# A hybrid trunk block on one core: 512-column products in the value projections, the FFN and the down projection

## The chip, the cores and the metric

The kernel runs on one core of one Trainium2 chip. The metric is the device time of one execution in microseconds (us), as the median of several runs. One run is also recorded by the hardware profiler, and its trace is read below.

## The reference, cut to what matters

One layer over 256 tokens of width 1024, batch 1, in float32. One input projection of the normed input feeds four token mixers and their gates; the gated mixers are summed and projected, and a SwiGLU FFN follows.

```
h = rmsnorm(x, norm_mix)
z, xbc, dt, qkvB, qkvC, f, qD, kvD, gates = split(h @ w_in)      # w_in: 1024 x 9488
A = mamba2(z, xbc, dt)            # 8 heads of 64, state 128, one chunk of 256 tokens
B = moba(qB, kB, vB, bias)        # 8 heads of 64; causal attention with a relative bias
C = fox(qC, kC, vC, f)            # 8 heads; logits less a running sum of log forget gates
D = swa(qD, kD, vD, bias, sinks)  # window of 128
m = sum over b of sigmoid(gate_b) * (branch_b @ w_branch[b])
x = x + m @ w_out
u = rmsnorm(x, norm_ffn)
x = x + (silu(u @ w_gate) * (u @ w_up)) @ w_down                 # width 2816
out = rmsnorm(x, norm_final)
```

## The kernel before

**Products in parts.** Each float32 operand of a projection is split into a high part and a low part, and a product becomes three: hi\*hi, hi\*lo and lo\*hi. The names of the parts end in h and l (xh, xl: the normed input; x2h, x2l: the FFN's input; ah, al: the FFN's inner activations) or begin with hi and lo (the weights). `three` (line 259) writes the list of terms. Before the change each of the three is an instruction of its own.

**Weight stream.** Weights come from DRAM in 1 MB pieces, in the order of `stream()`: the pieces of FIRST, then gates (g) and branch projections (wb), the output projection (wo), 22 FFN pieces (gu) and 11 pieces of the down projection (dn). SyncE (SP) issues the loads into three buffers `raw`; ScalarE (ACT) copies the high part (line 299) and VectorE (DVE) subtracts for the low part (line 307), each in two cuts. A piece of FIRST, and one of gu, holds 256 columns over the whole contraction of 1024. Its products run on TensorE (PE) as two halves of 24 products with 256 columns each (line 249 in the input projection, line 1106 in the FFN). A gate piece holds 512 columns over half the contraction, and its products are 512 columns wide (line 961). A piece of the down projection makes, for the first 128 tokens, two products of 512 columns, and for the second 512, 256 and 256 (line 1131).

**Side work.** Everything else (convolution, attention, norms, ends of the pieces) is written as generators. The `Weaver` (line 92) advances them between the halves of the projections, by rough costs and flags such as `"qkB0"` or `"erow"`. So the order on every engine is fixed when the program is built, and an engine whose next instruction waits holds all that stands behind it. A pair of heads in `att_pair` (line 720) goes through logits s on PE (lines 731, 733), bias and minimum on DVE (spB, lines 744 and 746), exponentials on ACT (pB), scaling on DVE, transposes on PE (ptB, line 776), copies on ACT (ptsB, line 782), and the product with the values on PE (yB, lines 652 and 654). MoBA's bias rows go through DRAM: ACT copies them (es), SP writes them (erow), and GpSimd (POOL) reads them back per pair (bB, line 557). They become due by this line:

```
    wv.later(lambda: bias_rows(), ["dt"])
```

The flag dt is raised where `softplus_cums` (line 484) is written out; its chain of some twenty small POOL instructions (lines 503 to 524) stands ahead of the bB reads in POOL's own queue.

**FFN end.** `end_ffn` (line 1076) scales both halves of a piece by 1/rms (gs, on DVE, 512 columns), takes the SiLU (sg, ACT), multiplies (DVE), and splits the result into ah (ACT) and al (DVE).

Of the kernel before, what the change touches and what calls it, by code (L numbers as in the profile page):

```python
# [15 lines left out]
EPS = 1e-6  # L16

# Columns of w_in.
# [20 lines left out]
def in_proj_pieces():  # L39
    """(name, columns of w_in) of each piece of the input projection."""  # L40
# [6 lines left out]
    for j in range(2):  # L47
        cols["xbc%d" % (2 + j)] = rng(XS0 + 256 * j, 256)
        cols["z%d" % j] = rng(Z0 + 256 * j, 256)
        cols["vB%d" % j] = rng(BV0 + 256 * j, 256)  # L50
        cols["vC%d" % j] = rng(CV0 + 256 * j, 256)
        cols["qD%d" % j] = dq[256 * j : 256 * j + 256]
# [18 lines left out]
WARM = 8  # L71
SLACK = 3500
# [5 lines left out]
class Need:  # L78
    """What a step of side work takes: rough times on the engines, and buffers by their tags."""
# [12 lines left out]
class Weaver:  # L92
    """Weaves side work into the instruction order of the projections.

    The projections keep the tensor engine busy; between two of their accumulation groups the steps of
    the other work are traced, as far as rough clocks of the engines say that they will not hold it up."""
# [16 lines left out]
    def step(self, t):  # L113
        """Run the task's next step if it fits; whether it did."""
# [49 lines left out]
    def tick(self, cost, last=True):  # L164
        """After a projection's group, or a part of one, that holds the tensor engine for cost."""
# [10 lines left out]
    def until_free(self, tag):  # L176
        """Trace side work until a buffer of this tag is free."""
# [8 lines left out]
    def until(self, flags):  # L186
        """Trace side work until these flags are up."""
# [10 lines left out]
def hybrid_block_kernel(ctx: ExitStack, tc: tile.TileContext, A, out):  # L198
# [45 lines left out]

    def group(o, terms):
        """One accumulation group; the groups of a bank follow each other."""
        n = len(terms)
        for j, (l, r) in enumerate(terms):
            pe.matmul(o, l, r, start=j == 0, stop=j == n - 1)  # L249

    def woven(o, terms, cuts=1):
        """One accumulation group with side work between its cuts."""
        n = len(terms)
        for j, (l, r) in enumerate(terms):
            pe.matmul(o, l, r, start=j == 0, stop=j == n - 1)  # L255
# [3 lines left out]
    def three(w, x, ks, wt, cuts=1):  # L259
        """Terms hi*hi + hi*lo + lo*hi; wt: the weights stand still (else the activations do)."""  # L260
        (wh, wl), (xh, xl) = w, x
        t = []
        step = len(ks) // cuts
        for a in range(0, len(ks), step):
            kk = ks[a : a + step]
            for k in kk:
                t += [(wh(k), xh(k)), (wh(k), xl(k))]
            t += [(wl(k), xh(k)) for k in kk]
        return t if wt else [(b, a) for a, b in t]
# [5 lines left out]
    names = stream()  # L275
    sizes = {n: 8 * len(c) for n, c in in_proj_pieces()}
# [25 lines left out]
    def split_lo(name, c, cuts):  # L302
        """After the last cut, the load of a later piece."""
# [10 lines left out]
    # The cuts of the splits in order; the first parts run one cut ahead of the second.  # L314
# [4 lines left out]
    def split_next(which, least, most):  # L319
        """Trace cuts of one of the two parts up to piece least, and one more cut up to piece most."""  # L320
# [68 lines left out]
    xh = [slot("xh%d" % i, dt=F32R) for i in range(2)]  # L389
    xl = [slot("xl%d" % i, dt=F32R) for i in range(2)]  # L390
# [7 lines left out]
    for a, b in chunks:  # L398
        for k in range(a, b):
            act.activation(xh[k // 4][:, k % 4, :], xT[k // 4][:, k % 4, :], AF.Copy, scale=nm_mix[:, k : k + 1])  # L400
        act.activation(hb[:, a:b, :], wb[:, a:b, :], AF.Copy)
        for k in range(a, b):
            dve.scalar_tensor_tensor(xl[k // 4][:, k % 4, :], xT[k // 4][:, k % 4, :], nm_mix[:, k : k + 1],
                                     xh[k // 4][:, k % 4, :].bitcast(F32), ALU.mult, ALU.subtract)
        dve.tensor_tensor(lb[:, a:b, :], wb[:, a:b, :], hb[:, a:b, :].bitcast(F32), ALU.subtract)
        for w, x in ((hb, xh), (hb, xl), (lb, xh)):
            for k in range(a, b):
                for j in range(2):
                    pe.matmul(px[j], w[:, k, tok(j)], x[k // 4][:, k % 4, :], start=k == 0 and w is hb and x is xh,
# [10 lines left out]
    def rms(name, ss, width):  # L420
        """(ss / width + eps) ** -0.5 of a [128, n] tile of sums of squares."""
# [7 lines left out]
    def rms_row(name, r):  # L429
        """The [128, 2] columns of 1/rms as one row on every partition, in PSUM [128, 256]."""  # L430
# [6 lines left out]
    def nat_groups(name, hi, lo, n=256):  # L437
        """n columns, natural layout: PSUM [128, 2 token halves, 256], or two banks."""
# [5 lines left out]
        for t in range(2):  # L444
            group(p[:, t, :] if n == 256 else p[t],
                  three((lambda k: hb[:, k, :], lambda k: lb[:, k, :]),
                                    (lambda k: xh[k // 4][:, k % 4, tok(t)],
# [815 lines left out]
```

## Time and profile before

| what | value |
|---|---|
| median of three runs | 523.21 us (522.54 to 524.31) |
| profiled execution, span | 522.5 us |
| PE busy | 512.6 us, 98% |
| DVE, ACT, POOL busy | 342.4, 272.6, 31.0 us |
| weights and data read | 94.46 MB, 183 GB/s over the span |

The profiled execution's own time is its span, 0.7 us under the median and just under the fastest of the three runs. PE is busy in all slices but the first and the last. The other engines have idle time, which costs nothing unless PE waits for them.

### The profile page before, as it was taken

Reading aid. Unit: us, or ns where it says so; the run is one execution under the profiler, and the core shown is the slowest. Engines: PE = TensorE matmul, PEld = TensorE weight load, DVE = VectorE, ACT = ScalarE, POOL = GpSimd, SP = SyncE. Lnnn points to the kernel's source line nnn. Section 1 sums busy time; section 2 is a strip of 40 time slices with the busy share of each in tenths; the row PEclk is TensorE's granted clock in tenths of the full one; section 3 lists DMA queues with packets and bytes.
Section 4 is the critical chain, followed back from the end, with each engine's and each line's share of the span. In section 5 each row is a group of like instructions: output and inputs, shape, how many; then the busy total and the mean of one; then the engine's idle time right before and its main releaser. Section 6 shows DMA issues by size and latency. Waiting matters only on the chain.

```text
span 522.5 us, 8748 instructions
## 1 busy us (share of the span) xinstructions
PE 512.6 (98%) x3544; PEld 467.2 (89%) x3544; DVE 342.4 (66%) x624; ACT 272.6 (52%) x471; POOL 31.0 (6%) x61
## 2 busy tenths in 40 slices
PE   7999999999999999999999999999999999999995
PEld 7999999898987778888888899999999999988884
DVE  4478887897968937547295495656656665673435
ACT  6576674665675853443534454755544544443412
POOL 2008110011200000000000000000000000000001
PEclk8999999999999999999999999999999999999999
DMA  7974665553563244726447282446455545575302
GB/s 232 378 266 156 202 208 180 190 149 150 188 215 123 82 161 167 273 109 258 162 161 279 113 327 88 166 162 238 162 173 212 181 162 181 216 289 181 141 1 83
DMA packets 17126, 96.13 MB, mean 184 GB/s; under 512 B 2235, under 2 KB 3563, under 8 KB 6844
## 3 DMA queue, kind: packets, MB, share of 16 engines
q1 hardware_dynamic: 15660, 91.15, 48.0%
q0 software_dynamic: 1424, 4.41, 3.1%
q8 instruction: 28, 0.46, 0.3%
q14 instruction: 14, 0.11, 0.1%
HBM read 94.46 MB, written 1.09 MB: 183 GB/s over the span
## 4 chain that ended last, share of the span: by engine, by line
PE 94%; DMA 3%; issue 1%; SPq 1%; DVE 0%; ACT 0%; POOL 0%; POOLq 0%; ACTq 0%
PE gu L1106 24%; PE pg L961 17%; PE pd L1131 11%; PE pb L255 8%; PE qkC L249 4%; PE qkB L249 4%; PE po L1062 4%; PE xbc L249 3%; DMA raw_xbc<-in_w_dram 3%; PE vC L249 2%; PE qD L249 2%; PE vB L249 2%; PE z L249 2%; PE n L249 1%; PE ptC L776 1%
## 5 line engine op out<-in xcount | busy, mean ns | idle before, releaser
L1106 PE MATMUL gu<-x2h,hi_gu 128*128 128x256 f32 x352 | 87.0, 283 | 0.0
L1106 PE MATMUL gu<-x2l,hi_gu 128*128 128x256 f32 x352 | 86.9, 283 | 0.0
L1106 PEld LDWEIGHTS gu<-x2l,hi_gu 128*128 128x128 f32 x352 | 67.6, 192 | 0.0
L1106 PEld LDWEIGHTS gu<-x2h,hi_gu 128*128 128x128 f32 x352 | 67.6, 192 | 0.0
L307 DVE TENSOR_TENSOR lo_gu<-raw_gu,hi_gu 128x1024 fp32r<-128x1024 f32 x44 | 53.2, 1217 | 1.4 <-ACT hi_gu L299 1.4
L1106 PE MATMUL gu<-x2h,lo_gu 128*128 128x256 f32 x352 | 51.4, 283 | 0.0
L961 PE MATMUL pg<-hi_g,xh 128*128 128x512 f32 x128 | 50.8, 397 | 0.0
L961 PE MATMUL pg<-hi_g,xl 128*128 128x512 f32 x128 | 50.0, 390 | 0.0
L299 ACT ACTIVATE hi_g<-raw_g 128x1024 fp32r<-128x1024 f32 x32 | 32.8, 1053 | 26.8 <-DMA raw_g<-in_w_dram 14.0
L1106 PEld LDWEIGHTS gu<-x2h,lo_gu 128*128 128x128 f32 x352 | 46.3, 192 | 0.0
L299 ACT ACTIVATE hi_gu<-raw_gu 128x1024 fp32r<-128x1024 f32 x44 | 45.4, 1049 | 1.6 <-PE gu L1106 1.6
L307 DVE TENSOR_TENSOR lo_g<-raw_g,hi_g 128x1024 fp32r<-128x1024 f32 x32 | 38.1, 1219 | 8.8 <-ACT hi_g L299 8.8
L1079 DVE TENSOR_TENSOR gs<-gu,rb2b 128x512 f32<-128x512 f32 x22 | 15.1, 690 | 43.9 <-PE gu L1106 43.9
L307 DVE TENSOR_TENSOR lo_dn<-raw_dn,hi_dn 128x1024 fp32r<-128x1024 f32 x22 | 26.1, 1220 | 22.7 <-ACT hi_dn L299 22.7
L1082 ACT ACTIVATE sg<-gs 128x256 f32<-128x256 f32 x22 | 9.1, 419 | 57.9 <-DVE gs L1079 57.9
L1131 PE MATMUL pd<-hi_dn,al 128*128 128x512 f32 (+1 forms) x110 | 37.3, 348 | 0.0
L1131 PE MATMUL pd<-hi_dn,ah 128*128 128x512 f32 (+1 forms) x110 | 37.2, 347 | 0.0
L299 ACT ACTIVATE hi_dn<-raw_dn 128x1024 fp32r<-128x1024 f32 x22 | 22.4, 1051 | 26.4 <-PE pd L1131 24.6
L961 PE MATMUL pg<-lo_g,xh 128*128 128x512 f32 x128 | 34.3, 389 | 0.0
L961 PEld LDWEIGHTS pg<-hi_g,xh 128*128 128x128 f32 x128 | 24.0, 188 | 6.3 <-issue 1.5
L1131 PE MATMUL pd<-lo_dn,ah 128*128 128x512 f32 (+1 forms) x110 | 29.2, 347 | 0.0
L961 PEld LDWEIGHTS pg<-lo_g,xh 128*128 128x128 f32 x128 | 24.0, 188 | 5.1
(332 smaller groups left out, 1201.8 us busy)
## 6 DMA issues: line engine op xcount, KB each, us to landing
raw_gu<-in_w_dram SPq DMA_DIRECT2D x22, 1024.0 KB, 4.8
raw_g<-in_w_dram SPq DMA_DIRECT2D x16, 1024.0 KB, 4.7
raw_dn<-in_w_dram SPq DMA_DIRECT2D x11, 1024.0 KB, 4.8
raw_wb<-in_w_dram SPq DMA_DIRECT2D x8, 1024.0 KB, 4.8
raw_qkB<-in_w_dram SPq DMA_DIRECT2D x4, 1024.0 KB, 5.2
raw_qkC<-in_w_dram SPq DMA_DIRECT2D x4, 1024.0 KB, 4.9
raw_wo<-in_w_dram SPq DMA_DIRECT2D x4, 1024.0 KB, 5.2
raw_vB<-in_w_dram SPq DMA_DIRECT2D x2, 1024.0 KB, 4.8
```

The source lines that it names most:

```text
L249: pe.matmul(o, l, r, start=j == 0, stop=j == n - 1)
L255: pe.matmul(o, l, r, start=j == 0, stop=j == n - 1)
L299: act.activation(parts[name][0][:, s], raws[name][:, s], AF.Copy)
L307: dve.tensor_tensor(lo[:, s], raws[name][:, s], hi[:, s].bitcast(F32), ALU.subtract)
L776: pe.transpose(pt[:, tok(c)], pp[i][:, tok(c)], ident)
L961: pe.matmul(pg[t], l, r, start=kh == 0 and i == 0, stop=kh == 1 and i == len(terms) - 1)
L1062: pe.matmul(po[m], l, r, start=kh == 0 and i == 0, stop=kh == 1 and i == len(terms) - 1)
L1079: dve.tensor_tensor(s, p, rb2b.broadcast_to([128, 2, 256]), ALU.mult)
L1082: act.activation(sg, s[:, 0, :], AF.Silu)
L1106: pe.matmul(p[:, j, :], l, r, start=ks[0] == 0 and i == 0, stop=ks[-1] == 7 and i == len(terms) - 1)
L1131: pe.matmul(pd[t, i], l, r, start=c == 0 and j == 0, stop=c == 10 and j == len(terms) - 1)
```

## The change

**FFN.** For pieces 4 to 21 the input is normed before its products: `normed_x2` makes, for each eighth of the contraction, x2T times norm_ffn times 1/rms, and splits it into x3x, a tile that holds the high and the low part next to each other. `wide` multiplies the high weights by both parts in one product of 512 columns, then the low weights by the high part in 256 columns. The two halves of the 512 columns are added at the end: ACT copies one half out of PSUM (ge), DVE adds the other (gs). Gate and up columns of a piece now have a bank each.

**Values.** A value piece is now half the contraction and 512 columns, like a gate's. Both pieces of a branch stand next to each other in FIRST, and a pair of heads waits for both.

**Down projection.** In pieces 0 to 8 the second 128 tokens also take two products of 512 columns. The last 256 columns of pieces 9 and 10 go into a bank of their own and are added at the end.

**Layout.** The tiles x, y, m, x2 and a hold both parts next to each other; where the products stay as they were, `mm` still issues two of 256 columns.

```diff
-FIRST = ("xbc0 xbc1 n0 qkB0 vB0 xbc2 qkB1 xbc3 vB1 z0 qkB2 z1 qkB3 qD0 qkC0 vC0 qkC1 qD1 qkC2 vC1 qkC3").split()
+FIRST = ("xbc0 xbc1 n0 qkB0 vB0 vB1 xbc2 qkB1 xbc3 z0 qkB2 z1 qkB3 qD0 qkC0 vC0 vC1 qkC1 qD1 qkC2 qkC3").split()
...
+RAW_F = 4
...
+    def wide(o, w, x, ks, start, stop):
+        (wh, wl), n = w, len(ks)
+        for i, k in enumerate(ks):
+            pe.matmul(o, wh(k), x(k), start=start and i == 0, stop=False)
+        for i, k in enumerate(ks):
+            pe.matmul(o[:, 0, :], wl(k), x(k)[:, 0, :], start=False, stop=stop and i == n - 1)
...
+    def normed_x2(k):
+        yield Need(dve=400, act=310, w1=1)
...
+        u = work("x3_%d" % k, [128, 256], "w1")
+        dve.scalar_tensor_tensor(u, x2T[k // 4][:, k % 4, :], nm_ffn[:, k : k + 1], rb2b[:, 0, :], ALU.mult, ALU.mult)
+        h_, l_ = (parts_of(x3x)(k)[:, i, :] for i in range(2))
+        act.activation(h_, u, AF.Copy)
+        yield Need(dve=340)
+        dve.tensor_tensor(l_, u, h_.bitcast(F32), ALU.subtract)
...
     def end_ffn(f, p):
...
+        if f < RAW_F:
+            dve.tensor_tensor(s, p, rb2b.broadcast_to([128, 2, 256]), ALU.mult)
+            rel(acc=1)
+        else:
+            e = work("ge%d" % f, [128, 2, 256], "w2")
+            for j in range(2):
+                act.activation(e[:, j, :], p[j][:, 1, :], AF.Copy)
+                dve.tensor_tensor(s[:, j, :], p[j][:, 0, :], e[:, j, :], ALU.add)
+            rel(acc=1, att=1, w2=1)
...
+        if f >= RAW_F:
+            if f == RAW_F:
+                wv.until(["x3_%d" % k for k in range(8)])
+            p = [(acc, att)[j]("gu%d%d" % (f, j), [128, 2, 256]) for j in range(2)]
+            for j in range(2):
+                wide(p[j], (lambda k: hb[:, k, tok(j)], lambda k: lb[:, k, tok(j)]), parts_of(x3x), range(8), True, True)
+                wv.tick(GROUP)
+            wv.tasks.append(Task(end_ffn(f, p), True))
+            continue
...
         for t in range(2):
-            for i in range(len(pdw[t])):
-                down(c, t, i)
+            for c0 in (0, 512):
+                if c == 0:
+                    pd[t, c0] = att("pd%d%d" % (t, c0), [128, 512])
+                down(c, t, c0, 512, pd[t, c0], c == 0, False)
             wv.tick(GROUP)
...
+            e = c0 + bank.shape[-1]
+            dve.tensor_tensor(y[:, c0:e], bank, y[:, c0:e], ALU.add)
```

The order of the instructions moves at three places that matter below. The first is DVE around the first pair of MoBA heads: spB is the bias step, lo_... the low part of a weight piece, cu, cc and bc the convolution. Before, these rows stand there:

```order
L307 TENSOR_TENSOR lo_vB_661<-raw_vB_497,hi_vB_660 128x1024
L531 COPY cumn<-cum_n 128x32
L576 SCALAR_TENSOR_TENSOR bc_225<-cu_520,cc_523 128x512
L582 MEMSET cu_825 128x2x3
L584 TENSOR_TENSOR cu_825<-xbc_711,rb 128x2x256
L576 SCALAR_TENSOR_TENSOR xs<-cu_655,cc_658 128x512
L307 TENSOR_TENSOR lo_z_741<-raw_z_617,hi_z_740 128x1024 x2
L744 ISA spB_870,nmB_871<-sB_751,bB_747 128x256
```

With the change the same step follows these:

```order
L609 SCALAR_TENSOR_TENSOR bc_224<-cu_477,cc_481 128x512
L615 MEMSET cu_692 128x2x3
L617 TENSOR_TENSOR cu_692<-xbc_581,rb 128x2x256
L339 TENSOR_TENSOR lo_xbc_609<-raw_xbc_474,hi_xbc_608 128x1024
L609 SCALAR_TENSOR_TENSOR bc_225<-cu_497,cc_500 128x512
L777 ISA spB_705,nmB_706<-sB_661,bB_657 128x256
```

The first bias step moves ahead: it now stands right behind the low part of xbc3's first half, before cumn, the convolution xs of xbc2 and the low parts of z0, which came earlier before.

The second place is ACT around the end of piece z0 (zt is its tanh; hi_qkB a high part of qkB3; ptsB the second pair's copies for its product with the values). Before:

```order
L618 ACTIVATE zt_1025<-zh_1023 128x512
L299 ACTIVATE hi_qkB_1029<-raw_qkB_864 128x1024
L782 ACTIVATE ptsB_1032<-ptB_985 128x384
L782 ACTIVATE ptsB_1034<-ptB_989 128x384
L299 ACTIVATE hi_qkB_1029<-raw_qkB_864 128x1024
```

With the change:

```order
L651 ACTIVATE zt_987<-zh_985 128x512
L331 ACTIVATE hi_qkB_992<-raw_qkB_840 128x1024
L638 ACTIVATE cu_889<-cc_892 128x2x256
L331 ACTIVATE hi_qkB_992<-raw_qkB_840 128x1024
L815 ACTIVATE ptsB_1041<-ptB_995 128x384
L815 ACTIVATE ptsB_1043<-ptB_999 128x384
```

The two copies move behind the convolution's tanh of xbc3 (cu) and the second cut of the high part.

The third place is PE in an FFN piece (gu). Before, high and low part of the input alternate under the same weights, and the low weights follow (the end of one half):

```order
L1106 MATMUL gu_3916<-x2h_3271,hi_gu_3819 128x256
L1106 MATMUL gu_3916<-x2l_3273,hi_gu_3819 128x256
L1106 MATMUL gu_3916<-x2h_3270,lo_gu_3820 128x256 x4
L1106 MATMUL gu_3916<-x2h_3271,lo_gu_3820 128x256 x4
L1106 MATMUL gu_3980<-x2h_3270,hi_gu_3883 128x256
```

With the change one half of a piece reads:

```order
L260 MATMUL gu_3781<-x3x_3682,hi_gu_3643 128x512 x2
L260 MATMUL gu_3781<-x3x_3683,hi_gu_3643 128x512 x2
L260 MATMUL gu_3781<-x3x_3684,hi_gu_3643 128x512 x2
L260 MATMUL gu_3781<-x3x_3685,hi_gu_3643 128x512 x2
L262 MATMUL gu_3781<-x3x_3682,lo_gu_3644 128x256 x2
L262 MATMUL gu_3781<-x3x_3683,lo_gu_3644 128x256 x2
L262 MATMUL gu_3781<-x3x_3684,lo_gu_3644 128x256 x2
L262 MATMUL gu_3781<-x3x_3685,lo_gu_3644 128x256 x2
```

Sixteen products of 256 columns have become eight of 512; the eight with the low weights stay.

## Rows read from the trace of the kernel before

**Rows 1.** The page's fourth part: shares of the chain that ended last.

```profile
PE 94%; DMA 3%; issue 1%; SPq 1%; DVE 0%; ACT 0%; POOL 0%; POOLq 0%; ACTq 0%
```

**Rows 2.** That chain in order of time: start us, us, engine and line, instructions.

```profile
39.72 5.76 PE xbc L249 x48
...
46.59 5.76 PE qkB L249 x48
...
67.37 0.44 PE xct L640 x4
...
236.95 21.76 PE pg L961 x96
...
333.99 121.67 PE gu L1106 x1014
455.66 55.34 PE pd L1131 x294
```

**Rows 3.** The same chain between 106 and 126 us, around attention products.

```profile
106.58 0.66 PE ptB L776 x6
107.23 2.87 PE qkC L249 x24
110.10 0.42 PE sB L731 x4
...
110.96 3.06 PE vC L249 x24
...
125.10 0.81 PE ptB L776 x6
```

**Rows 4.** Timeline of POOL: start us, us, instruction, and the wait before it.

```profile
45.68 0.25 POOL L514 TENSOR_TENSOR sp_p<-sp_p,sp_t 128x32 f32<-128x32 f32 x1
...
46.39 1.05 POOL L514 TENSOR_TENSOR sp_p<-sp_p,sp_t 128x32 f32<-128x32 f32 x1
...
52.81 0.20 POOL L524 COPY av<-dt 128x16 f32<-128x16 f32 x1
55.14 1.54 POOL L557 DMA_DIRECT2D bB<-erow  x2 [2.13 <-DMA erow<-es]
```

**Rows 5.** View of the tile bB, MoBA's bias rows: its reader on DVE, its transfers.

```profile
L744 DVE CUSTOM_DVE_ANT_0 spB<-sB,bB x8: 415/418/426, 63.2 to 113.9; 128x256 f32<-128x256 f32 x8
...
DMA to landing us min/median/max: 3.7/3.9/5.2
```

**Rows 6.** Timeline of ACT, 52 to 77 us.

```profile
52.95 0.97 ACT L480 ACTIVATE es<-e 8x384 f32<-8x384 f32 x2
...
70.45 0.63 ACT L605 ACTIVATE cu<-cc 128x512 f32<-128x512 f32 x1 [0.16 <-ACT pB L751]
...
74.86 1.04 ACT L299 ACTIVATE hi_qkB<-raw_qkB 128x1024 fp32r<-128x1024 f32 x1
75.81 0.85 ACT L782 ACTIVATE ptsB<-ptB 128x384 f32<-128x384 f32 x2
```

**Rows 7.** Timeline of DVE, 46 to 84 us.

```profile
46.12 1.22 DVE L307 TENSOR_TENSOR lo_xbc<-raw_xbc,hi_xbc 128x1024 fp32r<-128x1024 f32 x1
47.25 1.67 DVE L603 SCALAR_TENSOR_TENSOR cc<-cu,tapsh,cc 128x256 f32<-128x256 f32 x4
...
82.71 0.87 DVE L643 TENSOR_TENSOR xc<-xct,dt 128x128 f32<-128x128 f32 x4
```

**Rows 8.** Timeline of DVE at the start of the FFN.

```profile
340.26 1.28 DVE L1079 TENSOR_TENSOR gs<-gu,rb2b 128x512 f32<-128x512 f32 x2
...
349.00 1.09 DVE L1088 TENSOR_TENSOR al<-sg,ah 128x256 fp32r<-128x256 f32 x3
...
352.02 0.69 DVE L1079 TENSOR_TENSOR gs<-gu,rb2b 128x512 f32<-128x512 f32 x1 [0.79 <-PE gu L1106]
```

**Rows 9.** Timeline of ACT at the start of the FFN.

```profile
342.28 1.28 ACT L1082 ACT_TABLE_LOAD   x1
```

**Rows 10.** Sixteen FFN pieces: length, then busy us (instructions) of PE, PEld, DVE, ACT, POOL; clock, DMA.

```profile
352.00:444.20 92.20, 92.20 (x770) 92.20 (x770) 58.08 (x81) 43.84 (x64) 0.00 (x0) 1.00 0.52 186
```

More of the change, by code (lines that the diff above doesn't have):

```diff
@@ L254, in woven, with three, two @@
         for j, (l, r) in enumerate(terms):
-            pe.matmul(o, l, r, start=j == 0, stop=j == n - 1)
+            mm(o, l, r, j == 0, j == n - 1)
             if (j + 1) % (n // cuts) == 0:
                 wv.tick(GROUP / cuts, j == n - 1)
-    def three(w, x, ks, wt, cuts=1):
-        (wh, wl), (xh, xl) = w, x
+    def three(w, x, ks):
+        (wh, wl) = w
+        t = []
+        for k in ks:
+            t += [(x(k)[:, 0, :], wh(k)), (x(k)[:, 1, :], wh(k))]
+        return t + [(x(k)[:, 0, :], wl(k)) for k in ks]
+    def two(w, x, ks, cuts=1):
+        (wh, wl) = w
         t = []
@@ L455, in tr_groups @@
         for j in range(n // 128):
-            group(p[:, j, :], three((lambda k: hb[:, k, tok(j)], lambda k: lb[:, k, tok(j)]),
-                                    (lambda k: xh[k // 4][:, k % 4, :], lambda k: xl[k // 4][:, k % 4, :]),
-                                    range(8), True, cuts))
+            group(p[:, j, :], two((lambda k: hb[:, k, tok(j)], lambda k: lb[:, k, tok(j)]), xx, range(8), cuts))
             yield p
@@ L568, in hybrid_block_kernel, with yh, yl @@
     sqa = slot("sqa")
-    yh, yl = {}, {}
+    yy = {}
     def new_y(br):
-        yh[br], yl[br] = slot("yh" + br, dt=F32R), slot("yl" + br, dt=F32R)
+        yy[br] = [slot("y%s%d" % (br, i), (128, 2, 2, 256), F32R) for i in range(2)]
+    def yh(br, j):
+        return yy[br][j // 2][:, j % 2, 0, :]
+    def yl(br, j):
+        return yy[br][j // 2][:, j % 2, 1, :]
     def half_silu(o, h, th):
@@ L850, in end_scaled, with end_v @@
         wv.done.add(name)
-    def end_nat(name, outs, p):
-        yield Need(act=720)
-        for t in range(2):
-            act.activation(outs[t], p[:, t, :], AF.Copy, scale=r1[:, t : t + 1])
+    def end_v(br, t, p):
+        yield Need(act=620)
+        if br not in v:
+            v[br] = slot("v" + br, (128, 2, 512))
+        act.activation(v[br][:, t, :], p, AF.Copy, scale=r1[:, t : t + 1])
         rel(acc=1)
-        wv.done.add(name)
+        wv.done.add("v%s%d" % (br, t))
     def end_of(name, p):
@@ L909, in merged_parts @@
     def merged_parts(nh):
-        mth[nh], mtl[nh] = slot("mth%d" % nh, dt=F32R), slot("mtl%d" % nh, dt=F32R)
+        for kp in range(2):
+            mtx[2 * nh + kp] = slot("mtx%d%d" % (nh, kp), (128, 2, 2, 256), F32R)
         tps = []
@@ L1103, in hybrid_block_kernel @@
                 wv.until(["x2_%d" % k for k in ks])
-                terms = three(w, x, ks, True)
+                terms = two(w, x2x, ks)
                 for i, (l, r) in enumerate(terms):
-                    pe.matmul(p[:, j, :], l, r, start=ks[0] == 0 and i == 0, stop=ks[-1] == 7 and i == len(terms) - 1)
+                    mm(p[:, j, :], l, r, ks[0] == 0 and i == 0, ks[-1] == 7 and i == len(terms) - 1)
                 wv.tick(GROUP * len(ks) // 8, ks[-1] == 7)
@@ L1111, in hybrid_block_kernel @@
                 wv.tasks.append(Task(end_ffn(f_, gu[f_]), True))
+            for k in range(8):
+                wv.tasks.append(Task(normed_x2(k), True))
         gu[f] = p
@@ L1145, in hybrid_block_kernel @@
         o = slot("out%d" % t, (128, 1024))
-        ms, last = EPS, len(pdw[t]) - 1
-        for i, (c0, n) in enumerate(pdw[t]):
+        ends = (((0, 512), (512, 512)), ((0, 512), (512, 256), (768, 256)))[t]
+        ms, last = EPS, len(ends) - 1
+        for i, (c0, n) in enumerate(ends):
             ns = slice(c0, c0 + n)
+            bank = pd[t, c0] if c0 < 768 else att("pd_end", [128, 256])
             for c in (9, 10):
-                down(c, t, i)
+                down(c, t, c0, n, bank[:, :n], c == 9 and c0 == 768, c == 10)
             m = const("ms3_%d%d" % (t, i), [128, 1])
```

131 lines of the change are left out of this document (63 added, 68 removed).

## The prediction

> **What bounds the kernel now.** I read the chain that ended last first. PE holds 94% of it [rows 1], and its pieces follow each other without a gap: the FFN is one piece of 1,014 products, the down projection one of 294 [rows 2]. The windows view says the same of sixteen FFN pieces: PE is busy for all of 92.20 us, at full clock, while DVE works 58.08 and ACT 43.84 of them [rows 10]. So a product that becomes cheaper shortens the time at once, as long as no other engine makes PE wait; a wait that PE does not have today costs its full length. The prediction is therefore a sum of PE's products and of new waits. I looked for these by walking through the changed order with the durations of the trace.
>
> **Products: the gain.** The chain gives two prices. A run of 48 products of 256 columns takes 5.76 us, 120.0 ns each; 96 of 512 columns take 21.76 us, 226.7 ns each [rows 2]. Two of 256 cost 240.0, so one of 512 in their place saves 13.3 ns. The new wide products have weights in the stationary place and the activations moving, the gates' the other way round. The trace has no wide product of that kind, but 256-column products cost the same both ways: 121.67 us for 1,014 in the FFN is 120.0 each [rows 2]. So I take 13.3.
>
> Counted in the two orders, 438 pairs are merged: 288 in the FFN (18 pieces, two halves, 8 pairs), 96 in the four value pieces, 54 in the down projection. 438 x 13.3 ns is 5.83 us: 3.84, 1.28 and 0.72. The bounds are nothing (the saving would be gone if the fixed part belonged to each 256 columns and not to each instruction, which the gates' row contradicts) and 5.83.
>
> **Switches: a small gain.** After logits or a product with values, the next half of 24 products takes 3.06 us instead of 2.87, and a transpose for attention 0.81 instead of 0.66 [rows 3]. The cause is not shown; the price is 0.19 and 0.15. The changed order puts these products next to each other more often. Of logits followed by a projection there are 12 before and after; of value products followed by a projection 7 before and 6 after, by a transpose 6 before and 3 after. That is one of 0.19 and three of 0.15: 0.64 us. Bounds: 0 to 0.64.
>
> **Start of the FFN: covered.** Piece gu4 needs x3x, so 1/rms must be there and 24 new instructions must be done while PE works on gu3. Piece gu3 ends at 352.02, where DVE was waiting for it, and DVE began the first scaling at 340.26 [rows 8]. From there DVE has in the new order, by pitches from start to next start: two scalings at 0.6 (1.28 for two), eight products at 0.40 (cc, 1.67 for four [rows 7]), twelve instructions of 0.335 (al, 1.09 for three [rows 8]: eight low parts, two products, two al), and two cuts of the weights at 1.13 [rows 7]. That is 1.2 + 3.2 + 4.0 + 2.3 = 10.7. It waits about 1.7 for the first SiLU, since ACT loads a table for 1.28 until 343.56 [rows 9]. The last low part stands at about 352.7. PE needs it for the eighth product of gu4, at 352.02 + 7 x 0.227 = 353.6. Cost 0, with 0.9 us of cover; were 2 us more of work in the way, PE would lose 1.1, once.
>
> **Later FFN pieces: covered.** A piece gets shorter, 5.76 to 5.55. DVE has 58.08 / 16 = 3.63 us of work in one and ACT 2.74 [rows 10]. ACT gets two copies of 0.335 more, DVE two additions for one scaling, 0.07 more. 3.7 and 3.4 fit in 5.55, and PE has banks for the next pieces while an end is at work. Cost 0.
>
> **First MoBA pair: a new wait at the head of DVE's queue.** In the first order shown the bias step spB comes earlier. What it reads, bB, cannot come as much earlier. Before, POOL finished its chain at 53.01 and then waited for the rows in DRAM, issued at 55.14, and the transfer landed 3.9 us later (3.7 to 5.2 over the four [rows 5]), at 59.0; DVE read it at 63.2 [rows 4, 5]. With the change es, which ended at 53.92 [rows 6], is copied while PE works on xbc2, by about 49 (an estimate), so only POOL's chain holds the read: issue at about 53.05, landing at 56.95. DVE gets there sooner. The two value pieces in a row begin at 33.96 (one piece before 39.72) and take 48 x 0.227 = 10.9; 1.1 of side products (45.48 to 46.59) and xbc2's 5.76 put its end at 51.7 [rows 2]. One scaling, one cut, one bc later, 2.4 us, DVE stands at spB: 54.1. It waits 2.9 us.
>
> Behind it in DVE's order stand the other cut of xbc3, cumn (PE transposes it and POOL reads its rows for the Mamba pairs), the scaling of pB, and the convolution of xbc2; ACT's tanh of that, a cut and the running sums stand ahead of the copies ptsB. From 56.95 I add on DVE 1.1 for the bias steps [rows 5], 1.13, 0.1, 1.3 for pB (an estimate: six small instructions at 0.2 to 0.3), 0.6, six convolution steps at 0.40 and one cut: 64.7; on ACT tanh 0.54, cut 0.95, row copy 0.3 and two copies of 0.42 [rows 6]: 67.4. PE reaches the first product with the values after four halves (3.06 + 3 x 2.87) and 3.6 of side products at the prices of rows like these [rows 2, 3]: 51.7 + 15.3 = 67.0. So PE waits 0.4. With landing 0.2 earlier it is 0.2, with 5.2 for the transfer 1.7. I take 0.4.
>
> **Second MoBA pair: ACT's copies come late.** In the second order shown both ptsB stand behind tanh cu and a cut. From the end T of z0 on PE, DVE has a scaling 0.6, two convolution steps 0.8, a cut 1.13, four xc 0.85, zs 0.6 and four steps 1.65 [rows 7, 8]: 5.6. Then ACT: tanh 0.55, cut 0.95, two copies 0.85 [rows 6]: T + 8.0. PE has transposes for xc 0.44, two halves of 2.87 and ptB 0.66 [rows 2, 3]: T + 6.8. It waits 1.2 by this, and less where ACT's rows overlap more; I take 1.0, bounds 0.6 to 1.25. Later, one pair of the FoX branch (sC3) comes close as well: 0.25, bounds 0 to 0.35.
>
> **Down projection and end.** One addition on DVE near the end grows from 256 to 512 columns, 0.3 us more, in front of the last one, which waited for PE by about as much. I take 0; bound 0.3.
>
> **Sum.** -5.83 - 0.64 + 0.4 + 1.0 + 0.25 = -4.8. The profiled execution is 522.5, so its like is 517.7; the median is 0.7 above that execution, so the forecast is 518.4. With every bound at its best it is 517.5, with the worst (no switches saved, waits of 1.7, 1.25 and 0.35, tail 0.3) 521.0.
>
> **Rivals.** Differences under about 0.3%, 1.6 us, can hardly be told from no change here: faster means under 521.6, slower over 524.8.
>
> *B, the bias rows come later still.* POOL's chain is sensitive: one of its instructions takes 0.25 us at 45.68 and 1.05 at 46.39, while DVE subtracts a low part at 46.12 [rows 4, 7]. With one or two more such meetings, or a slow transfer, landing moves from 56.95 to 58.5 or 60, and everything behind the bias step moves with it: PE waits 2 to 3.5 instead of 0.4, and the Mamba pairs, which need cumn, may add 0.5. That gives 520.0 to 522.0. Against it: the number of cuts on DVE during the chain is the same before and after. The Trainium skill (SBUF — State Buffer, section "SBUF: two separate sides") has a rule for this: VectorE with two inputs in SBUF and a GpSimd instruction that reads it exclude each other for a whole instruction. By that rule a cut that starts first costs POOL up to its whole 1.1 us; the trace agrees, with 0.8 more.
>
> *C, the saving is not in the instruction.* If a product of 512 in the FFN ran at twice the price of 256, only the switches and the waits would remain: 522.5 - 0.64 + 1.65 + 0.7 = 524.2; with a fifth of the saving left, 523.1. The Trainium skill (TensorE: Matmul & The Clock Gate, section "Back-to-back issue gap") speaks for such a small saving: its gap between products is a term in the columns plus 2.5 ns, so that a merged pair would save 2.5 and not 13.3 ns, 1.1 us in all, an estimate by that page. The trace does not agree: its two prices, 120.0 and 226.7, leave 13.3 for each instruction.
>
> *D, slower: each wide piece has to wait.* A piece now needs two banks, and its end passes between ACT and DVE twice more (ge, then gs). If the banks come free late, PE waits once per piece. From 0.38 us per piece on, 17 x 0.38 = 6.4 takes back all that products and switches save beyond the other waits, 6.5 - 1.65, and another 1.6; at 0.45 it is 526.0 and slower than before. It needs ACT or DVE to have more than 5.55 us of work per piece, or the end to take over a piece's length before it lets go of a bank. The rows say 3.7, and about 1.4 up to the release (two copies, two additions); hence a small chance.
>
> **How the numbers follow.** The sum holds with 0.67 (516.9 to 519.8). B has 0.16, most of it still faster: 0.13, and 0.03 no change. C 0.06, no change. D 0.08, slower; it stands for any wait in the FFN that the walk missed, since 18 pieces repeat it. The last 0.03 is that PE's waits don't come and more is saved: under 516.9. The range from 516.9 to 521.2 holds the first case and nearly all of B, 0.8. Faster: 0.67 + 0.03 + 0.13 = 0.83; same: 0.06 + 0.03 = 0.09; slower: 0.08.
>
> **What would show it.** Right: wide products at 227 ns in the FFN's chain, a piece in 5.55 us, no wait of PE between 352 and the end; DVE idle for about 3 us at its first spB, released by the transfer of bB; PE waiting twice for ptsB, for half a microsecond at about 67 and one at about 82. Wrong: a wide product over 235 ns (C), idle time of PE before gu rows (D or the start), a first spB later than 58 us (B).

## The result, and the profile after

The change took 519.50 us (median of four, 519.36 to 521.76) beside 523.76 for the kernel before: ratio 0.9925, 95% interval 0.9908 to 0.9941, so 3.9 us faster by the ratio (3.1 to 4.8 by its interval) and 4.3 by the medians. The forecast was 518.4 with a range of 516.9 to 521.2. Timed once more in another set, it took 521.72 (nine runs, 518.33 to 522.92) beside 523.89, ratio 0.9950, 0.9934 to 0.9967. That is 2.2 us faster by the medians, and 0.5 above the forecast's range. Why it differs so from run to run is the subject of half of what follows.

The profiled execution has a span of 517.8 us, and its time is 519.55. The chain after, in order of time (start us, us, engine and line, instructions), at the places of [rows 2]; the first row, which has its fellow in the row from the kernel before below it, is the first piece whose products are the same in both:

```profile
21.10 6.02 PE n L250 x48
33.10 10.91 PE pvB L989 x48
...
351.32 1.84 PE gu L260 x8
353.16 0.95 PE gu L262 x8
...
451.88 54.44 PE pd L1186 x240
```

The same row of the kernel before:

```profile
21.97 6.02 PE n L249 x48
```

The reader is to see three things. The profiled execution of the change is 0.87 us ahead before its first changed instruction: the first loads landed earlier, which differs from run to run (that row begins between 21.1 and 22.7 in the profiles of this study). So of the 4.7 us between the two spans only 3.8 belong to the change. The value pieces run at 10.91 / 48 = 227.3 ns a product and the down projection at 54.44 / 240 = 226.8, the gates' price of [rows 2]. The FFN's wide products do not: 1.84 for eight is 230.

The list of PE's waits in the execution after (what waited, for what: us in total, times, longest; the list leaves out waits under 0.15 us), and the windows view of the 18 pieces, as in [rows 10]:

```profile
PE xbc L440 <- ACT hi_xbc L432: 2.3, 2, 2.1
PE warm L424 <- DVE cumu L383: 1.1, 1, 1.1
PE yB L685 <- ACT ptsB L815: 0.9, 1, 0.9
```

```profile
352.00:451.90 99.90, 99.90 (x575) 87.97 (x574) 69.67 (x112) 59.57 (x109) 0.00 (x0) 1.00 0.54 191
```

PE waits once after the start, for the second pair's copies, as forecast. In the FFN it never waits here; DVE has 69.67 / 18 = 3.9 us of work per piece and ACT 3.3, close to what was worked out (3.7 and 3.4).

The first MoBA pair: timelines of POOL and DVE (start us, us, instruction, and the wait before it), which answer to [rows 4]:

```profile
51.39 0.20 POOL L551 COPY av<-dt 128x16 f32<-128x16 f32 x1
51.54 1.54 POOL L584 DMA_DIRECT2D bB<-erow  x2
```

```profile
46.50 1.27 DVE L339 TENSOR_TENSOR lo_qkB<-raw_qkB,hi_qkB 128x1024 fp32r<-128x1024 f32 x1
...
55.98 0.42 DVE L777 CUSTOM_DVE_ANT_0 spB<-sB,bB 128x256 f32<-128x256 f32 x1 [2.66 <-DMA bB<-erow]
```

POOL no longer waits for the rows in DRAM (2.13 us before): its own chain, which ends at 51.59, is what holds the read, and DVE stands 2.66 us at the head of its queue. The forecast said 2.9. The second pair, on ACT's timeline, as in [rows 6]:

```profile
79.94 0.64 ACT L638 ACTIVATE cu<-cc 128x512 f32<-128x512 f32 x1 [3.36 <-issue]
80.48 1.04 ACT L331 ACTIVATE hi_qkB<-raw_qkB 128x1024 fp32r<-128x1024 f32 x1
81.42 0.85 ACT L815 ACTIVATE ptsB<-ptB 128x384 f32<-128x384 f32 x2
```

ACT is idle for 3.36 us ahead of the convolution's tanh (cu), with the two copies behind it, for which PE waits. The row names no releaser; DVE's last steps of that convolution end at 79.85, 0.09 before the tanh begins:

```profile
78.19 1.66 DVE L636 SCALAR_TENSOR_TENSOR cc<-cu,tapsh,cc 128x256 f32<-128x256 f32 x4
```

### The profile page after: what moved, and what is told of

It reads as the page before. It is cut to its first block, busy times and chain, and to the rows that moved or that the text cites. A ratio compares the mean times of both kernels' runs of the same rounds, so it can differ in the third digit from the quotient of the medians.

```text
span 517.8 us, 7989 instructions
## 1 busy us (share of the span) xinstructions
PE 507.6 (98%) x3106; PEld 444.1 (86%) x3106; DVE 350.6 (68%) x658; ACT 284.1 (55%) x511; POOL 29.7 (6%) x61
## 4 chain that ended last, share of the span: by engine, by line
PE 95%; issue 2%; DMA 1%; ACT 1%; DVE 1%; SPq 0%; POOL 0%; POOLq 0%; ACTq 0%; DVEq 0%
PE pg L989 17%; PE gu L260 13%; PE pd L1186 11%; PE pb L250 8%; PE gu L262 7%; PE pvC L989 2%; PE pvB L989 2%; PE qkC L252 2%; PE po L250 1%; PE gu L250 1%; PE gu L253 1%; PE po L253 1%; PE gu L252 1%; PE qkC L250 1%; PE po L252 1%
## 5 line engine op out<-in xcount | busy, mean ns | idle before, releaser
L260 PE MATMUL gu<-x3x,hi_gu 128*128 128x512 f32 x288 | 72.1, 392 | 0.0
L989 PE MATMUL pg<-hi_g,xx 128*128 128x512 f32 x256 | 64.3, 393 | 0.0
L260 PEld LDWEIGHTS gu<-x3x,hi_gu 128*128 128x128 f32 x288 | 51.8, 189 | 9.3
L989 PEld LDWEIGHTS pg<-hi_g,xx 128*128 128x128 f32 x256 | 47.4, 188 | 11.1 <-issue 1.5
L1186 PE MATMUL pd<-hi_dn,aa 128*128 128x512 f32 (+1 forms) x176 | 46.2, 384 | 0.0
L262 PEld LDWEIGHTS gu<-x3x,lo_gu 128*128 128x128 f32 x288 | 39.3, 190 | 2.8
L262 PE MATMUL gu<-x3x,lo_gu 128*128 128x256 f32 x288 | 40.2, 282 | 0.0
L1186 PEld LDWEIGHTS pd<-hi_dn,aa 128*128 128x128 f32 x176 | 32.6, 188 | 6.5
L989 PE MATMUL pg<-lo_g,xx 128*128 128x512 f32 x128 | 34.3, 389 | 0.0
L1186 PE MATMUL pd<-lo_dn,aa 128*128 128x512 f32 (+1 forms) x88 | 26.7, 384 | 0.0
```

Of the source, the lines that this page charges most:

```text
L260: pe.matmul(o, wh(k), x(k), start=start and i == 0, stop=False)
L262: pe.matmul(o[:, 0, :], wl(k), x(k)[:, 0, :], start=False, stop=stop and i == n - 1)
L989: pe.matmul(pg[t], l, r, start=kh == 0 and i == 0, stop=kh == 1 and i == len(terms) - 1)
L1186: pe.matmul(o, l, r, start=start and j == 0, stop=stop and j == len(terms) - 1)
```

## The experiments

All comparisons below by trace are of stretches of PE's work, since the start differs by more than some of the effects. They are: from the first product of piece n to the first of the FFN; from there to the first product of the down projection; and the rest of PE's work. What follows PE's last product is not in the table; it takes 5.9 to 6.0 us in ten profiles and 6.7 in those of e5, e7 and e10, which is taken up at the end of this section. The kernels were timed in four sets, each beside its own runs of the kernel before (medians 523.76, 523.95 for e1 to e4, 524.04 for e5 to e8, 523.89 for e9 to e11), so a ratio says more than a median. "Lost at gu4" is how much longer the first wide products of the FFN take than the same products of later pieces.

| kernel | median us, n | ratio to before (95%) | n to FFN | FFN | rest | lost at gu4 |
|---|---|---|---|---|---|---|
| before | - | - | 305.92 | 127.78 | 61.07 | - |
| the change | 519.50, 4 | 0.9925 (0.9908 to 0.9941) | 306.11 | 124.66 | 60.18 | 0 |
| e1_no_wide_ffn | 523.67, 11 | 0.9994 (0.9986 to 1.0003) | 306.04 | 127.78 | 60.18 | - |
| e2_no_wide_values | 519.75, 6 | 0.9923 (0.9911 to 0.9934) | 306.10 | 124.66 | 60.17 | 0 |
| e3_hi_then_lo | 519.83, 6 | 0.9928 (0.9909 to 0.9946) | 305.84 | 124.86 | 60.18 | 0.6 |
| e4_early_pts | 519.24, 5 | 0.9907 (0.9893 to 0.9920) | 306.98 | 125.92 | 60.18 | 1.3 |
| e5_bias_on_sp | 520.43, 5 | 0.9933 (0.9920 to 0.9946) | 305.73 | 125.71 | 60.18 | 1.0 |
| e6_late_gu4_split | 519.95, 5 | 0.9922 (0.9909 to 0.9936) | 307.60 | 124.66 | 60.18 | 0 |
| e7_all_mended | 518.97, 4 | 0.9901 (0.9887 to 0.9914) | 304.39 | 124.30 | 60.18 | 0 |
| e8_four_and_four | 520.95, 1 | - | 305.91 | 126.15 | 60.18 | 1.0 |
| e9_change_again | 521.72, 9 | 0.9950 (0.9934 to 0.9967) | 306.20 | 125.86 | 60.18 | 1.2 |
| e10_mended_again | 518.73, 4 | 0.9910 (0.9897 to 0.9923) | 304.40 | 124.30 | 60.18 | 0 |
| e11_moves_without_sp | 518.19, 4 | 0.9895 (0.9882 to 0.9908) | 304.68 | 124.30 | 60.17 | 0 |

**One part undone.** First the FFN, then the values.

```diff
-RAW_F = 4
+RAW_F = 22
...
-            for k in range(8):
-                wv.tasks.append(Task(normed_x2(k), True))
```

> The changed kernel with its FFN pieces 4 to 21 in 256 columns as before (no normed copy of the input, no second bank, no halves to add); values and down projection stay wide. Theory: the trace of the change shows 5.587 us per wide piece, so the FFN is worth 18 x 0.171 = 3.1 us and this kernel takes 519.5 + 3.1 = 522.6. By the sum on record (3.84 for the FFN) it takes 523.3. Rival: the new ends on ACT and DVE cost PE something elsewhere (start of the FFN, down projection), then less comes back than 3.1 and it takes under 522.

It took 523.67, no faster than before within its interval. By trace the FFN is 127.78 again, to the hundredth as before: the FFN is worth 3.12, not 3.84. The down projection keeps its 0.89, and the input projection stays 0.12 slower than before. So by trace 0.77 us should be left of the gain, where the medians of this set leave 0.3. The median is 1 us over the theory's 522.6; the difference between the sets (the change took 519.50 in one and 521.72 in another) is as large.

```diff
-FIRST = ("xbc0 xbc1 n0 qkB0 vB0 vB1 xbc2 qkB1 xbc3 z0 qkB2 z1 qkB3 qD0 qkC0 vC0 vC1 qkC1 qD1 qkC2 qkC3").split()
+FIRST = ("xbc0 xbc1 n0 qkB0 vB0 xbc2 qkB1 xbc3 vB1 z0 qkB2 z1 qkB3 qD0 qkC0 vC0 qkC1 qD1 qkC2 vC1 qkC3").split()
...
-        cols["vB%d" % j] = rng(BV0, 512)
-        cols["vC%d" % j] = rng(CV0, 512)
+        cols["vB%d" % j] = rng(BV0 + 256 * j, 256)
+        cols["vC%d" % j] = rng(CV0 + 256 * j, 256)
...
```

> The changed kernel with the value pieces as before: 256 columns over the whole contraction, at their old places in the order of pieces, each pair of heads waiting for its own half. FFN and down projection stay wide. Theory: the 1.28 us that the wide value products save, and about 0.25 of switches, are taken back by new waits of PE (0.3 at the first MoBA product with the values, 1.25 at the second, 0.15 at a FoX pair), so the time is the same within 0.4 us, 519.3, and PE waits for no ptsB. Rival: the waits come from other parts of the change and stay, then 1.5 us are lost: 521.0.

The theory holds: 306.10 with narrow values, 306.11 with wide ones, and in its list of PE's waits there is none for ptsB:

```profile
PE xbc L440 <- ACT hi_xbc L432: 2.9, 1, 2.9
PE warm L424 <- DVE cumu L383: 1.1, 1, 1.1
```

The value part of the change gains nothing: its cheaper products are paid back in waits. (This kernel is not the kernel before up to the FFN: it is 0.19 slower, all of it lost at one place, where cum_n follows the first half of xbc3. The cause of that was not looked into.)

**Why a wide product costs more in the FFN.** The next kernel runs the wide products of both halves first.

```diff
-            for j in range(2):
-                wide(p[j], (lambda k: hb[:, k, tok(j)], lambda k: lb[:, k, tok(j)]), parts_of(x3x), range(8), True, True)
-                wv.tick(GROUP)
+            x3 = parts_of(x3x)
+            for j in range(2):
+                for k in range(8):
+                    pe.matmul(p[j], hb[:, k, tok(j)], x3(k), start=k == 0, stop=False)
+            wv.tick(GROUP)
+            for j in range(2):
+                for k in range(8):
+                    pe.matmul(p[j][:, 0, :], lb[:, k, tok(j)], x3(k)[:, 0, :], start=False, stop=k == 7)
+            wv.tick(GROUP)
```

> The changed kernel with another order inside an FFN piece: the high weights of both halves first (16 products of 512 columns), then the low weights of both (16 of 256). Theory: a wide product costs 227 ns, but the first five after a run of 256-column products cost 27 ns more together, and the first narrow ones 7 less; with one such switch per piece instead of two the 18 pieces take 100.2 us instead of 100.56, and the run 519.15. Rival: 230 ns is the price of a wide product in the FFN whatever stands before it, then 100.56 and no change.

The chain of this kernel, at the start of piece gu4 and at one later:

```profile
351.32 4.21 PE gu L1153 x16
355.52 1.91 PE gu L1157 x16
...
385.27 3.65 PE gu L1153 x16
388.92 1.91 PE gu L1157 x16
```

A piece now takes 3.65 + 1.91 = 5.56, the change's 2 x (1.84 + 0.95) = 5.58 and, to the hundredth over 18 pieces, 100.56 / 18 = 5.587. With the 0.56 us at gu4 (4.21 instead of 3.65) taken off, the FFN is 124.30, 0.36 under the change: the size that was expected. The opposite move, four wide and four narrow in turns, is the second test:

```diff
-                wide(p[j], (lambda k: hb[:, k, tok(j)], lambda k: lb[:, k, tok(j)]), parts_of(x3x), range(8), True, True)
+                for a in (0, 4):
+                    wide(p[j], (lambda k: hb[:, k, tok(j)], lambda k: lb[:, k, tok(j)]), parts_of(x3x), rng(a, 4), a == 0, a == 4)
```

> The changed kernel with each half of an FFN piece in four runs: four wide products, four narrow, four wide, four narrow. Theory: each run of wide products after narrow ones costs about 23 ns more for its first four and the narrow ones 7 less; 36 more of them bring 18 pieces from 100.56 to 101.0 us. Rival (230 ns is the price of a wide product here): 100.56.

```profile
383.11 0.93 PE gu L260 x4
384.04 0.47 PE gu L262 x4
384.51 0.93 PE gu L260 x4
385.44 0.48 PE gu L262 x4
```

0.93 for four is 232.5 each, where a run of eight has 230 and a long run 227. By the starts of its products a piece takes 5.61, and 18 of them 0.5 more than the change's. The rival, a fixed price of 230, is out: the price of a wide product hangs on how recently narrow ones ran.

**The loss at gu4.** It was not looked for; it showed in the first row of e3 above and in the profiles of e4, e5, e8 and e9. The timelines of ACT and DVE in the change's own execution, the FFN's start:

```profile
339.59 2.01 ACT L331 ACTIVATE hi_gu<-raw_gu 128x1024 fp32r<-128x1024 f32 x2 [1.55 <-PE gu L253]
341.62 1.28 ACT L1131 ACT_TABLE_LOAD   x1
```

```profile
343.36 0.76 DVE L1133 TENSOR_TENSOR sg<-sg,gs 128x256 f32<-128x256 f32 x2 [1.70 <-ACT sg L1131]
...
350.70 1.42 DVE L1114 TENSOR_TENSOR x3x<-x,x3x 128x256 fp32r<-128x256 f32 x4
```

and the same two places in e3_hi_then_lo:

```profile
340.61 2.01 ACT L331 ACTIVATE hi_gu<-raw_gu 128x1024 fp32r<-128x1024 f32 x2 [2.56 <-DMA raw_gu<-in_w_dram]
342.63 1.28 ACT L1131 ACT_TABLE_LOAD   x1
```

```profile
344.38 0.76 DVE L1133 TENSOR_TENSOR sg<-sg,gs 128x256 f32<-128x256 f32 x2 [2.71 <-ACT sg L1131]
```

The high part of gu4's weights stands in ACT's queue ahead of the table load and the first SiLU. In e3 its load lands 1.0 us later, and everything behind it, x3x at the end, comes 1.0 later. In the change x3x is complete at 352.12, and PE asks for the last of it at 351.32 + 7 x 0.23 = 352.9. On paper 0.8 us of lateness are free; by e3, which is 1.0 late and loses 0.56, it is half a microsecond. In e9, the change again, ACT begins that copy at 342.52, 2.9 us later than here with everything else only 1.25 later, and PE's list of waits has:

```profile
PE yB L685 <- ACT ptsB L815: 0.9, 1, 0.9
PE gu L260 <- DVE x3x L1114: 0.6, 1, 0.6
```

(The 0.6 is the first wait; four of the next products follow at DVE's pace of 0.335 and lose another 0.1 each.) That the load is what is late is named in the rows of e3, e5 and e8; in e4 and e9 the row names a DVE step that ended just then, and the load's landing is not recorded. The test is to take the copy out of the way:

```diff
-        ahead[0] = 2
+        ahead[0] = 1 if f in (1, 2) else 2
```

> The changed kernel with the high part of FFN piece gu4 one step later in ACT's order, behind the table load and the first SiLUs. Theory: in the change that copy waits for its load from DRAM (up to 3.3 us in the profiles), and the whole chain to x3x stands behind it; in the executions where the load is late PE waits 0.5 to 0.7 us at gu4. With the move x3x is ready some 2 us earlier, no profile shows a wait at gu4, and the median is the same to 0.3 lower: 519.3. Rival: gu4's own weights now come late and PE waits for them: 520.5.

The low part of the piece, on DVE, moves with it. Its profile loses nothing at gu4 (124.66), and neither do those of the three kernels with more moves that contain it (e7, e10 and e11), where five of the seven profiles without it, of kernels with a wide FFN, lost 0.6 to 1.3. The last part of x3x is now there before the first product of gu4 and not 0.97 behind it as in the change (352.12, where the product itself begins at 351.15); in e6 it ends at 353.30, where that product begins at 354.11:

```profile
351.88 1.42 DVE L1114 TENSOR_TENSOR x3x<-x,x3x 128x256 fp32r<-128x256 f32 x4
```

The lead is 0.81 us in all four profiles. The median of e6, 519.95, is within the spread of the change's runs and shows no gain by itself; its profiled execution (522.51, the slowest of five) lost 2.3 us at the first two MoBA products, the case that was rival B:

```profile
PE yB L685 <- ACT ptsB L815: 2.3, 2, 1.4
```

Its timeline of POOL, end of the softplus chain and start of the bias rows:

```profile
53.00 1.30 POOL L548 TENSOR_SCALAR ea<-ea 128x8 f32<-128x8 f32 x1
...
55.11 1.54 POOL L584 DMA_DIRECT2D bB<-erow  x2
```

The same small instruction, line 548, took 0.24 in the change's profile and in that of e9; here it is 1.30, beside the first cut of xbc3's low part on DVE (52.98 to 54.20), and the rows are issued at 55.1, where the change has 51.5 and e9 52.7. What made POOL late is again a copy that waits for its load. The high part of xbc2 stands in ACT's queue ahead of the first steps of the softplus; it waited 2.87 us for its load in e6 and 3.02 in e4, against 0.98 in the change. (In e1 a wait of 2.54 us there still ended early enough.) The row of e4, and that of the change:

```profile
36.75 2.01 ACT L334 ACTIVATE hi_xbc<-raw_xbc 128x1024 fp32r<-128x1024 f32 x2 [3.02 <-DMA raw_xbc<-in_w_dram]
```

```profile
33.35 2.01 ACT L331 ACTIVATE hi_xbc<-raw_xbc 128x1024 fp32r<-128x1024 f32 x2 [0.98 <-DMA raw_xbc<-in_w_dram]
```

**The two MoBA waits.** A few rows of code bring the second pair's copies forward, and nothing else moves.

```diff
...
+        for t in [t for t in self.tasks if t.need.first and self.fits(t.need)]:
+            self.run(t)
         for t in [t for t in self.tasks if t.urgent]:
             self.advance(t)
...
-        yield Need(act=830, pt=2)
+        n = Need(act=830, pt=2)
+        n.first = br == "B" and j == 1
+        yield n
```

> The changed kernel with one move: the two copies ptsB of the second MoBA pair stand ahead of the convolution's tanh and the second cut of the high part on ACT, as before the change; nothing else moves on any engine. Theory: PE's wait of 0.9 us for ptsB at 81 us and about 0.3 inside that product with the values go, 1.2 us in all: 518.3. Rival: what is now behind the copies (tanh of xbc3, cut of qkB3) comes 0.8 later and PE waits for that instead, at xct or at qkB3: 519.5, no change.

The copies start at 80.27, as soon as PE has transposed, and PE's product follows without a wait:

```profile
80.27 0.88 ACT L820 ACTIVATE ptsB<-ptB 128x384 f32<-128x384 f32 x2 [1.33 <-PE ptB L812]
```

The median, 519.24, is 0.3 under the change's first and 2.5 under its second. But the profiled execution was the slowest of the five (521.86): POOL's chain ended late, the bias rows were there at 58.3, and PE lost 2.1 at the first pair's copies and 1.3 at gu4. The first of these is met by this:

```diff
...
-        return att_pair("B", j, (2 * j, 2 * j + 1), lambda: rows2("bB%d" % j, erow, 384, 2 * j, 1),
+        return att_pair("B", j, (2 * j, 2 * j + 1), lambda: rows2("bB%d" % j, erow, 384, 2 * j, 1, pool if j else nc.sync),
```

> The changed kernel with one transfer on another queue: the first pair's bias rows bB are issued by SP, behind the rows' own store, and no longer by POOL behind its softplus chain. Theory: the rows land at about 53, DVE no longer stands 2.7 us at the first spB, PE loses no 0.35 at the first product with the values; since ACT's order keeps the second pair's copies behind a tanh that hangs on z0's end, the 1.25 there stays: 519.2. In executions where POOL's chain starts late (2.1 us of wait in the profile of the early copies) that wait goes too. Rival: the 2.7 us are felt all the way down, the second pair's wait shrinks with them, and it takes 518.0; or SP, which now waits for the store's landing, holds the weight load behind it and nothing is won.

```profile
49.99 0.39 SPq L584 DMA_DIRECT2D bB<-erow  x1
```

```profile
55.51 0.42 DVE L777 CUSTOM_DVE_ANT_0 spB<-sB,bB 128x256 f32<-128x256 f32 x1 [1.60 <-DMA bB<-erow]
```

The rows landed at about 55.4, not 53: the transfer took 5.4 us. DVE still stands 1.6 instead of 2.7. Up to the FFN the kernel is 0.38 faster than the change by trace, as expected, with the wait of 0.9 in the second pair unchanged. Against that its profile loses 1.0 at gu4 and 0.78 behind PE's last product, and its median is 520.43 where 519.2 was expected. That the other runs lost at gu4 as well is not shown.

**All four moves, and three.**

> The changed kernel with the four moves together: copies of the second MoBA pair early, first bias rows on SP, high weights of both halves of an FFN piece first, gu4's high part later. Theory: 1.25 + 0.35 + 0.35 and up to 0.3 for the late loads are won: 517.4 (517.2 to 517.8), and PE waits nowhere after 30 us but for 0.15 at a FoX pair. Rival: the mended waits hand on to the next ones and less than half is won: 518.7.

> The change itself, once more, on the same chip as the next two. Theory: 3.9 us under the kernel before, 520.0 beside 523.9; in the profile the wait of 0.9 at the second MoBA product with the values, and at the first products of gu4 a loss between 0 and 1.2 us that goes with the landing of gu4's load. Rival: the run with no loss at gu4 was the rule and not the exception, then no loss there.

> The kernel with the four moves, once more, beside the change. Theory: 1.5 to 2.5 us under the change (1.72 in the input projection, 0.36 in the FFN, and what the change loses at gu4 in this set of runs), no wait of PE after 30 us. Rival: the difference in the medians is 0.5, as the two earlier medians have it, since other waits take up what is won.

> The kernel with three of the four moves: the first bias rows stay on POOL, behind the softplus chain. Theory: 0.35 over the kernel with all four where POOL's chain is in time, up to 2 us over it in executions where the chain starts late; median 0.4 over it. Rival: the move to SP costs SP as much as it gives, no difference.

The four moves are 1.72 us faster than the change up to the FFN and 0.36 in it, and in both profiles the list shows no wait of PE after 30 us; that of e10_mended_again:

```profile
PE xbc L443 <- ACT hi_xbc L435: 2.8, 3, 1.8
PE warm L427 <- DVE cumu L386: 1.1, 1, 1.1
PE xbc L255 <- ACT hi_xbc L334: 0.7, 1, 0.7
```

Timed with the change on one chip, they take 518.73 against 521.72, and three moves without SP's 518.19: intervals of the ratios 0.9897 to 0.9923, 0.9934 to 0.9967 and 0.9882 to 0.9908. Both beat the change and the kernel before. The difference to the change is larger than forecast in this set (3.0 us, where 1.5 to 2.5 was expected), since the change is slow in it. In the set before, e7 took 518.97 where 517.4 was expected, 0.5 under the change's first median.

**What the move to SP costs.** By the stretches of the table the bias rows on SP are worth 0.28 (304.40 against 304.68), and still e11, without them, has the lower median, against what was expected. The loss is behind PE's last product, outside the table. SP's waits at the end of the program, in e10 with the move and in e11 without it:

```profile
SPq L1333 <- DMA out_dram<-out: 1.7, 1, 1.7
```

```profile
SPq L1333 <- DMA out_dram<-out: 1.0, 2, 0.6
```

The program ends with SP waiting for a row of signals, most of them of transfers, in a fixed order. In both kernels the last piece of the output has landed 5.0 us after PE's last product. In e11 its signal is nearly the last in that order, and the other waits are done by then. With one more transfer on SP the output has another signal, which stands near the front of the order; SP waits there for 1.7 us and goes through the other signals only then. From PE's last product to the end it is 6.67 us in e10 and 5.89 in e11. The same 0.8 is in both other profiles with the move and in none without it. So the move to SP wins 0.28 and loses 0.78, 0.5 in all, and the medians differ by 0.54 the same way, though their intervals overlap. The three moves of e11 are the better kernel.

## Why the prediction came out, step by step

The sum was -4.8 and the change, by trace, is -3.8. The time of the first set fell into the range, that of the second did not. Three terms of the sum were too hopeful, by 0.7 (FFN), 0.35 (second MoBA pair) and 0.3 (switches); two came out 0.2 better each (down projection, FoX pair). That the profiled execution's span came out at 517.8, beside the 517.7 that the forecast has for its like, is luck: 0.87 of the difference is the start.

**Products.** Right in mechanism and in price for the values and the down projection (227.3 and 226.8). The term of 3.84 for the FFN was mis-sized: it is 3.12. The step that went wrong is "so I take 13.3" for wide products that alternate with narrow ones: each half of a piece goes once from narrow to wide and back, which costs 20 ns, and 36 such halves make the missing 0.72. The first wide products cost 233, 236, 228, 232 and 231 ns before the price settles at 227, and the first narrow one 113 instead of 120, by starts of PE's instructions in the change's FFN. The price stood in the trace of before: there the down projection changes between 18 wide and 12 narrow products, and the starts show 234, 236, 228, 232 and 231 ns, then 227, and 113 for the first narrow one. The two rows that the 13.3 was taken from are long runs of one width. Rival C, no saving in the instruction, is out: the merged pairs save 10.8 on the average in the FFN (3.12 us over 288), far from 2.5. (The Trainium skill, TensorE: Matmul & The Clock Gate, section "Back-to-back issue gap", gives 2.5 ns as the fixed part of the gap of an isolated product, and other figures for a stream; the traces here don't agree with the 2.5: it is 13.3 in long runs of either width.)

**Switches.** Mis-sized: 0.64 forecast, about 0.34 found, as a remainder. The stretch from the value pieces to the end of the first branch projection became 0.2 longer; with 1.28 of products saved and 1.82 of waits (next paragraph), the rest is -0.34. Where the other 0.3 went is not shown. The pairs' logits are not it: they stand right behind a product with values at five places now and at one before, but cost 0.86 us at either kind of place, in both traces.

**New waits.** Right in place and cause, and in size but for the second pair. First pair: 0.4 forecast, 0.38 found (its product with the values takes 1.17 instead of 0.80 and starts 0.01 late). Second pair: 1.0 forecast with bounds 0.6 to 1.25, 1.35 found: 0.97 ahead of it and 0.38 inside it (1.18 instead of 0.80), where the second head waits for its own copy. FoX pair: 0.25 forecast, 0.09 found (its logits take 0.94 instead of 0.86). The experiments bear out the first two: with the copies early, or with narrow values, the second wait is gone; with the bias rows on another queue the first one is, and the kernels with both moves win 1.72, close to 0.38 and 1.35 together.

**Start of the FFN.** "Covered, 0.9 us" was right for the profiled execution and wrong as a statement about runs. The 0.9 was worked out from one execution of before, in which the load of gu4 happened to land before ACT asked for it; nothing waited for that load then, so its lateness left no mark in the trace of before. The step named its own price (1.1 lost for 2 us more in the way), and about that was found: 1.2 and 1.3 with the copy some 1.7 us late against the rest. It can make about half of the difference between the change's two sets. In the one execution of the second set that was profiled the other half is the start, which is 1.2 us later than in the first set's; for the other runs both are open. The later pieces never wait; rival D is out.

**Rival B** is not a rival but a share of the runs: in two of the profiles, e4 and e6, the first pair's bias rows came late and PE lost 1.4 to 2.1 there. POOL's chain began 1.5 and 2.6 us later than in the change's profile, behind the copy of xbc2 that waited for its load, and it met DVE's cuts once more: 1.33 and 1.30 us for an instruction of 0.25 near its end, as the rival said. Where the chain is in time, two such meetings are seen as before; one takes 1.14 us beside the cut at 46.50 above. (The Trainium skill, SBUF — State Buffer, section "SBUF: two separate sides", has the exclusion of the two engines; the trace agrees, with 1.14 us for an instruction that takes 0.35 otherwise.)

**Down projection and end.** 0.72 forecast, 0.89 found: before, ten pieces changed from wide to narrow products and back, and that price, 20 ns each time, is gone too. No kernel here undoes this part alone; the 0.89 is read from the traces.

**The anchor.** The forecast was the median, 523.2, less the sum, and that holds: 523.2 - 3.8 is 519.4. But the profiled execution's time is not its span, and it was not just under the fastest run: in all runs on record but two of e1's (2.9 us) the time is 1.7 to 1.9 us over the span, so it took about 524.3, the slowest of the three.

## What to carry to other kernels

A product that is merged into a wider one is worth its whole fixed part (13.3 ns here) only within long runs of equal width, 10.8 in runs of eight: order the work so that wide products stand together. When a new piece of work is put on the critical path through engines that were off it, look for what already stands ahead of it in their queues, above all for copies that wait for a load: a wait that cost nothing in the profile of before leaves no trace of how late it can be. Compare effects of one or two microseconds by stretches of the trace and not by spans, when the first loads alone move a run by more than one, and let the stretches reach to the end of the execution: a transfer on another queue can cost more there than it won.

## What the runs showed of the hardware

The price of a 512-column product depends on what ran before it: 228 to 236 ns for the first five behind narrow ones, 227 from the sixth on, at full clock and with PE busy throughout (99.90 of 99.90 us). Two 64-row products of a pair of heads start within 10 ns of each other when both inputs are there (0.80 us for a pair's eight products); when the second is late the heads' products run one behind the other, and the eight take 1.17 to 1.18 us. The end of the program costs 0.8 us more when SP waits for the last store ahead of its other signals (e5, e7, e10).
